# Layer 1's S5 tables: a later start inside layer 0's MLP, and matrix parts that are issued 8 planner units behind their VectorE parts

## The chip, the cores and the metric

The kernel runs on one core of a Trainium2 chip. The metric is the device time of one execution in microseconds. Before the change it is 1744.45 us, the median of three runs (1743.82 to 1749.99). One further execution was recorded by the hardware profiler.

The core's engines run side by side, each through its own list of instructions in order: PE (TensorE, matrix products), DVE (VectorE), ACT (ScalarE), POOL (GpSimd) and SP (SyncE, which here only issues DMAs). They wait for one another through semaphores.

## The reference, cut to what matters

Two layers of a backbone work on 256 latent tokens and 256 context tokens of width 1024. Each layer has a token mixer with four branches, one of which is a bidirectional diagonal state-space mixer (S5), and then an MLP with squared ReLU. Layer 0 computes both token streams, layer 1 the latent one alone. All is in float32.

```python
def sq_relu_mlp(h, w1, w2):                  # w1 1024 x 4096, w2 4096 x 1024
    return jnp.square(jax.nn.relu(h @ w1)) @ w2

def s5_discretize(a_re, a_im, log_dt, b_re, b_im):
    ...
    mag = jnp.exp(lam_re * dt)
    lb_re = mag * jnp.cos(lam_im * dt)       # 16 groups x 64 states, two directions
    lb_im = mag * jnp.sin(lam_im * dt)
    ...
    bb_re = f_re[..., None] * b_re - f_im[..., None] * b_im
    bb_im = f_re[..., None] * b_im + f_im[..., None] * b_re
    return lb_re, lb_im, bb_re, bb_im
...
for l in range(DEPTH):
    mod = jax.nn.silu(c) @ ada_w[l] + ada_b[l]        # adaLN: 1024 x 6144 per layer
    ...
    y, y_c = token_mixer(h, hc, need_ctx, w_in[l], ...)
    x = x + g1 * rms_norm(y, norm_gains[l, 1])
    x = x + g2 * rms_norm(sq_relu_mlp(h, mlp_w1[l], mlp_w2[l]), norm_gains[l, 3])
```

The S5 recurrence runs in blocks of 8 tokens in the kernel. That needs tables, made only from weights: powers of the state factors times B (into the state), powers times C (out of the state), and the response inside a block. They depend on no token and must be in memory when a layer's S5 mixer reads them.

## The kernel before, in words

**Weight tiles.** Every large matrix comes as tiles of 128 x 1024 floats (512 KB). SP loads a tile into `wstage` (three buffers). ACT rounds it to the fast float32r format (`whi`, line 224), DVE computes the rest (`wlo`, line 206), and both are prepared two tiles ahead of their use (four buffers each). PE then runs 24 products of 128 x 128 by 128 x 512 per tile (line 217): 8 blocks of the inner dimension, times three combinations of high and low parts.

**Layer 0's MLP.** Four rounds q = 0 to 3. A round takes 8 tiles of w1 (numbers 8q to 8q+7), whose results pass through `hidden`: ACT makes ReLU, square and the high part, DVE the low part `flo`. Then it takes 8 tiles of w2, whose results DVE adds into `y`. The first four w1 tiles and the last four w2 tiles are done in two halves of 256 columns. Between these, in the fixed list of jobs, stand 48 tiles of `ada_w` for later adaLN vectors: after the first 12 jobs of the stage, 8 ada tiles behind 8 weight tiles, then two weight tiles without. An ada tile is multiplied on DVE by the condition and summed into `aacc` (lines 209 and 213): two operations per tile for layer 0's last part and layer 1's first two parts (24 tiles), one operation per tile for layer 1's other three (24 tiles), by the `conds` of line 406. After each 8 there is a short sum on PE (line 380).

**Side work and its clock.** Small chains of work are Python generators, here `s5_tables(1, ...)` for layer 1. The kernel's author keeps a planner clock. A 512-column weight tile calls `tick` 8 times with 0.648 each, between its blocks. A started generator is resumed at the first tick at which its due time has passed; each resumption adds 0.5 to the clock and sets the due time to the yielded number later. So a yield of 0, 1, 2, 3 or 8 is worth 1, 2, 4, 5 or 13 ticks. This gives the program order. The framework then orders each engine's instructions by that order and by a simulated readiness, so that an instruction whose inputs are there can be moved ahead onto an idle engine. `drain()` runs whatever is left of the generators before the last four w2 tiles.

**The tables of one layer.** `s5_tables` loads B and C (`bct`), makes phases on POOL (`s5_phases`), copies powers on ACT into `pb` and `pc` (line 647), and scales `pb` on DVE. For layer 1 these copies are put behind the instruction `behind` on ACT, which is the ReLU of the w1 tile before the start. Then:

- Four steps make the tables into the state. A step has two halves (real, imaginary): three DVE operations into `raw` (one buffer), four PE transposes (line 679), an ACT copy into `sti` (line 681). Behind the step stands a DMA of 512 KB, then a yield.
- Four steps make the tables out of the state: six small and three large DVE operations and four large POOL operations into `bb` and `sto`, a DMA of 512 KB, a yield; then twice POOL memsets and ACT copies into `ct` and eight PE instructions (line 717), an ACT copy and four small DMAs, a yield.
- At the end 16 gathering loads into `TP` and two stores.

In the kernel before, the generator starts before w1 tile 12.

Of the kernel before, what the change touches and what calls it, by code (L numbers as in the profile page):

```python
# [196 lines left out]
def _emit(tc, I, out):  # L197
# [4 lines left out]
    def act(o, i, f, **k):  # L202
        return S.activation(o, i, f, **k)  # L203

    def tt(o, a, b, op, eng=None):
        return (eng or V).tensor_tensor(o, a, b, op=op)  # L206
# [4 lines left out]
    def ts(o, a, s1, s2, op0, op1=None, eng=None):  # L211
        if op1 is None:
            return (eng or V).tensor_scalar(o, a, s1, None, op0=op0)
        return (eng or V).tensor_scalar(o, a, s1, s2, op0=op0, op1=op1)
# [45 lines left out]
    with es:  # L260
# [53 lines left out]
        def start(gen, delay=0.0, first=False):  # L314
            rec = [gen, clock[0] + delay, first]
            active.append(rec)
            return rec
# [188 lines left out]
        def dense(job, ahi, alo, n):  # L506

            w = next_job(job)
            ps = dense_ps()
            product(ps, w, ahi, alo, 0, n)  # L510
            return ps

        def dense_group(group, ahi, alo, l):

            ws = [next_job(j) for j in group]
            for c0, n, sel in halves(l):
                for i in range(len(ws)):
                    ps = dense_ps()
                    product(ps, ws[i], ahi, alo, c0, n)
                    yield i, sel, ps[:, :n]  # L520
# [108 lines left out]
        def s5_tables(l, tp, keep_in=None, behind=None):  # L629
# [35 lines left out]
            def rank1(o, pw, vec, gs, eng=None):  # L665
                tt(o, pw[:, gs, :, None].to_broadcast([128, 4, 8, 16]),
                   vec[:, gs, None, :].to_broadcast([128, 4, 8, 16]), MUL, eng)
            vb, vc = bcv[:, 0], bcv[:, 1]
            for q in range(4):
                gs = slice(4 * q, 4 * q + 4)  # L670
                raw = tp.tile([128, 2, 4, 8, 16], F32, name="raw", tag="raw")
                sti = tp.tile([128, 4, 2, 128], F32, name="sti", tag="sti", bufs=1 if keep_in is None else 4)
                for ri in range(2):
                    rank1(raw[:, ri], pb[:, 0], vb[:, ri], gs)
                    rank1(t4, pb[:, 1], vb[:, 1 - ri], gs)
                    tt(raw[:, ri], raw[:, ri], t4, (SUB, ADD)[ri])
                    ps = psm.tile([128, 512], F32, name="pm", tag="pm")
                    for g in range(4):
                        PE.transpose(ps[:, 128 * g:128 * g + 128],
                                     raw[:, ri, g].rearrange("p s c -> p (s c)"), ident)  # L680
                    S.copy(sti[:, :, ri], ps.rearrange("p (g m) -> p g m", g=4))
                if keep_in is None:
                    SP.dma_start(s5_dr[l][:, gs, 0:2], sti)
                else:
                    keep_in.append(sti)
                yield 2.0
            for q in range(4):
                gs = slice(4 * q, 4 * q + 4)
                f16 = [a[:, gs, None].to_broadcast([128, 4, 16]) for a in (fr, fi)]
                v1 = t1[:, 0:64].rearrange("p (g c) -> p g c", g=4)  # L690
                tt(bb[:, 0, :, 0:16], vb[:, 0, gs], f16[0], MUL)
                tt(v1, vb[:, 1, gs], f16[1], MUL)
                tt(bb[:, 0, :, 0:16], bb[:, 0, :, 0:16], v1, SUB)
                tt(bb[:, 1, :, 0:16], vb[:, 1, gs], f16[0], MUL)
                tt(v1, vb[:, 0, gs], f16[1], MUL)
                tt(bb[:, 1, :, 0:16], bb[:, 1, :, 0:16], v1, ADD)
                sto = tp.tile([128, 4, 2, 128], F32, name="sto", tag="sto")
                cp = [sto[:, :, i].rearrange("p g (s c) -> p g s c", s=8) for i in range(2)]
                rank1(cp[0], pc[:, 0], vc[:, 0], gs)
                rank1(t4, pc[:, 1], vc[:, 1], gs)  # L700
                tt(cp[0], cp[0], t4, SUB)
                rank1(cp[1], pc[:, 0], vc[:, 1], gs, G)
                rank1(t4b, pc[:, 1], vc[:, 0], gs, G)
                tt(cp[1], cp[1], t4b, ADD, G)
                ts(cp[1], cp[1], -1.0, None, MUL, eng=G)
                SP.dma_start(s5_dr[l][:, gs, 2:4], sto)
                yield 3.0
                ps = psm.tile([128, 512], F32, name="pm", tag="pm")
                for ri in range(2):
                    ct = tp.tile([128, 4, 15, 16], F32, name="ct", tag="ct")  # L710
                    G.memset(ct[0:64, :, 0:7, :], 0.0)
                    G.memset(ct[64:128, :, 8:15, :], 0.0)
                    act(ct[:, :, 7, :], vc[:, ri, gs], AF.Copy, scale=(1.0, -1.0)[ri])
                    S.copy(ct[0:64, :, 8:15, :], cp[ri][0:64, :, 0:7, :])
                    S.copy(ct[64:128, :, 0:7, :], cp[ri][64:128, :, 1:8, :])
                    for g in range(4):
                        PE.matmul(ps[32 * g:32 * g + 32, 0:240], bb[:, ri, g, :],
                                  ct[:, g].rearrange("p i c -> p (i c)"), start=(ri == 0), stop=(ri == 1))
                rsb = tp.tile([128, 240], F32, name="rsb", tag="rsb")
                S.copy(rsb, ps[:, 0:240])  # L720
                for g in range(4):
                    SP.dma_start(r_dr[l][4 * q + g], rsb[32 * g:32 * g + 16])
                yield 1.0
# [641 lines left out]
        SP.dma_start(smp, I["smp"].rearrange("l p n -> p l n"))  # L1365
        maps_in = []
        tables = s5_tables(0, pt, maps_in)
        next(tables)
        first_dma(1)
# [35 lines left out]
        for l in range(L):  # L1405
# [198 lines left out]
            def y_out(n, ps, c0, w, add, last):  # L1604
                o = y[:, n, c0:c0 + w]
                if add:
                    tt(o, o, ps, ADD)
                else:
                    S.copy(o, ps)
                if last:  # L1610
                    a = sqa[:, c0:c0 + w]
                    if n == 0:
                        act(a, o, AF.Square)
                    else:
                        q = px.tile([128, 512], F32, name="sq", tag="sq", bufs=2)
                        act(q[:, :w], o, AF.Square)
                        tt(a, a, q[:, :w], ADD)
# [9 lines left out]
            def hidden(j, ps, c0, w):  # L1627
                r = px.tile([128, 512], F32, name="hr", tag="hr", bufs=2)
                i = act(r[:, :w], ps, AF.Relu)
                r2 = px.tile([128, 512], F32, name="hq", tag="hq", bufs=2)  # L1630
                act(r2[:, :w], r[:, :w], AF.Square)
                split(fhi[:, j, c0:c0 + w], flo[:, j, c0:c0 + w], r2[:, :w])
                return i
# [16 lines left out]
            for q in range(4):  # L1650
                j0 = 0
                if q == 0:
                    j0 = g2
                    for i, sel, ps in dense_group([("w1", l, n) for n in range(g2)], hhi, hlo, l):
                        hidden(i, ps, 256 * sel, 256)
                for j in range(j0, 8):
                    if l == 0 and 8 * q + j == 12:
                        pt = Pool("pt1")
                        start(s5_tables(1, pt, None, gate))
                    gate = hidden(j, dense(("w1", l, 8 * q + j), hhi, hlo, nq)[:, :nq], 0, nq)  # L1660
                for n in range(8 - g3 if q == 3 else 8):
                    y_out(n, dense(("w2", l, 8 * q + n), fhi, flo, nq)[:, :nq], 0, nq, q > 0, q == 3)
# [28 lines left out]
```

## Time and profile before

| | us |
|---|---|
| median of the three runs | 1744.45 |
| the profiled execution | 1743.24 |
| its span from first to last instruction | 1741.4 |
| PE busy in the span | 1596.5 |
| DVE busy | 1083.1 |
| ACT busy | 796.8 |
| POOL busy | 219.9 |
| mean granted TensorE clock, share of full speed | 0.961 |

Times in the trace count from the start of the span. An engine's busy time is the sum of its instructions' times; a PE matmul's end is modelled, so PE's pace is better read from starts. "idle before" and the name behind an arrow say what ended an engine's idle time. PEclk is the granted TensorE clock of a stretch: 1.00 is 2.4 GHz, 0.50 would be 1.2 GHz all through, and a value between is a mixture of the two.

### The profile page before, as it was taken

The page shows a single profiled execution, that of the slowest core. Times are in us where ns is not written, and L with a number is a line of the kernel's source. Part 1 is how long each engine was busy: PE and PEld are TensorE (multiplying, and loading weights), DVE is VectorE, ACT ScalarE, POOL GpSimd, SP SyncE. Part 2 cuts the span into 40 slices and gives each one's busy share as a digit, 9 for nine tenths or more (in the row PEclk, how much of TensorE's full clock was granted, in tenths as well). Part 3 has the DMA queues.
Part 4 walks back from the last instruction along what each step waited for, and adds up shares of the span by engine and source line. Part 5 has one row for each costly group of instructions (what it writes and reads, how often), then busy time and mean ns, then how long its engine had stood idle before and what let it go on. Part 6 is the DMA issues. An engine that isn't in the chain of part 4 may idle for free.

```text
span 1741.4 us, 25278 instructions
## 1 busy us (share of the span) xinstructions
PE 1596.5 (92%) x9560; PEld 1320.0 (76%) x9560; DVE 1083.1 (62%) x1943; ACT 796.8 (46%) x1488; POOL 219.9 (13%) x316
## 2 busy tenths in 40 slices
PE   6699999999999798998799999889999887789996
PEld 2588767766778687876568888778888787779996
DVE  8765644475537668758844546684567675565554
ACT  5444455533334355524324244534775340556553
POOL 6730000000002373001310000100000030000000
PEclk9799999999999898999899999999999997889998
DMA  8446543554346532545565653436635550447552
GB/s 318 148 135 207 170 124 94 142 162 115 99 157 219 168 110 85 169 159 168 160 176 166 197 160 129 149 111 187 201 117 182 144 166 8 138 140 230 188 183 85
DMA packets 135913, 268.41 MB, mean 154 GB/s; under 512 B 38128, under 2 KB 76016, under 8 KB 135664
## 3 DMA queue, kind: packets, MB, share of 16 engines
q1 hardware_dynamic: 135792, 266.80, 48.9%
q8 instruction: 75, 1.23, 0.3%
q14 instruction: 46, 0.38, 0.1%
HBM read 234.02 MB, written 32.74 MB: 153 GB/s over the span
## 4 chain that ended last, share of the span: by engine, by line
PE 75%; DVE 12%; DMA 6%; ACT 3%; issue 3%; POOL 1%; SPq 0%; POOLq 0%; ACTq 0%; DVEq 0%
PE pd L217 39%; PE pm L217 23%; PE pg L217 9%; DVE wlo L206 2%; DMA wstage<-in_ada 1%; DMA wstage<-in_w 1%; DMA gin<-g_dr 1%; PE pm L833 1%; ACT whi L224 1%; PE pd L380 1%; DVE hlo L209 1%; DVE aacc L209 1%; DVE raw L206 1%; DVE gin L209 1%; DVE cv L209 1%
## 5 line engine op out<-in xcount | busy, mean ns | idle before, releaser
L206 DVE TENSOR_TENSOR wlo<-wstage,whi 128x1024 fp32r<-128x1024 f32 x264 | 327.1, 1241 | 257.6 <-ACT whi L224 240.7
L224 ACT CAST whi<-wstage 128x1024 fp32r<-128x1024 f32 x264 | 276.2, 1048 | 411.8 <-PE pd L217 163.3
L217 PE MATMUL pd<-hhi,whi 128*128 128x256 f32 (+1 forms) x1184 | 408.3, 346 | 20.9 <-ACT us L1425 11.1
L217 PE MATMUL pd<-hlo,whi 128*128 128x256 f32 (+1 forms) x1184 | 404.0, 342 | 5.7 <-DVE hlo L209 5.7
L217 PE MATMUL pd<-hhi,wlo 128*128 128x256 f32 (+1 forms) x1184 | 402.5, 341 | 1.3 <-DVE wlo L206 1.3
L217 PEld LDWEIGHTS pd<-hhi,whi 128*128 128x128 f32 x1184 | 225.3, 191 | 63.3 <-issue 13.4
L217 PEld LDWEIGHTS pd<-hlo,whi 128*128 128x128 f32 x1184 | 225.6, 191 | 38.6 <-issue 8.7
L217 PEld LDWEIGHTS pd<-hhi,wlo 128*128 128x128 f32 x1184 | 225.5, 191 | 31.7 <-issue 7.1
L217 PE MATMUL pm<-hhi,whi 128*128 128x256 f32 (+1 forms) x352 | 116.1, 331 | 6.3 <-ACT hhi L203 6.3
L217 PE MATMUL pm<-hlo,whi 128*128 128x256 f32 (+1 forms) x352 | 115.6, 329 | 3.9 <-DVE hlo L209 3.9
L209 DVE SCALAR_TENSOR_TENSOR aacc<-wstage,csl,aacc 128x1024 f32<-128x1024 f32 x70 | 88.6, 1284 | 46.2 <-DMA wstage<-in_ada 45.9
L217 PE MATMUL pm<-hhi,wlo 128*128 128x256 f32 (+1 forms) x352 | 114.9, 327 | 0.3 <-DVE wlo L206 0.3
L217 PE MATMUL pd<-fhi,wlo 128*128 128x256 f32 (+1 forms) x272 | 90.9, 334 | 2.8 <-DVE wlo L206 2.8
L217 PE MATMUL pd<-fhi,whi 128*128 128x256 f32 (+1 forms) x272 | 90.9, 335 | 2.5 <-DVE y L206 1.4
L217 PE MATMUL pm<-fhi,wlo 128*128 128x256 f32 (+1 forms) x272 | 89.6, 330 | 1.2 <-DVE wlo L206 1.2
L217 PE MATMUL pm<-fhi,whi 128*128 128x256 f32 (+1 forms) x272 | 90.1, 331 | 0.7 <-ACT fhi L224 0.7
L217 PE MATMUL pd<-flo,whi 128*128 128x256 f32 (+1 forms) x272 | 90.6, 333 | 0.0
L217 PE MATMUL pm<-flo,whi 128*128 128x256 f32 (+1 forms) x272 | 89.5, 329 | 0.0
L217 PEld LDWEIGHTS pm<-hhi,whi 128*128 128x128 f32 x352 | 68.7, 195 | 14.0 <-ACT hhi L203 8.0
L217 PEld LDWEIGHTS pm<-hlo,whi 128*128 128x128 f32 x352 | 68.1, 194 | 10.2 <-DVE hlo L209 4.8
L217 PEld LDWEIGHTS pm<-hhi,wlo 128*128 128x128 f32 x352 | 68.2, 194 | 6.0 <-DVE wlo L206 0.5
L1174 POOL MEMSET N<- 32x1024 f32 x8 | 7.6, 946 | 431.4 <-DMA n_dr<-N 222.9
(588 smaller groups left out, 2917.8 us busy)
## 6 DMA issues: line engine op xcount, KB each, us to landing
wstage<-in_w SPq DMA_DIRECT2D x128, 512.0 KB, 4.2
wstage<-in_win SPq DMA_DIRECT2D x104, 512.0 KB, 4.0
wstage<-in_ada SPq DMA_DIRECT2D x80, 512.0 KB, 3.6
ada<-in_ada SPq DMA_DIRECT2D x16, 512.0 KB, 10.5
g_dr<-gt SPq DMA_DIRECT2D x32, 256.0 KB, 3.1
gin<-g_dr SPq DMA_DIRECT2D x16, 512.0 KB, 4.1
wstage<-in_wb SPq DMA_DIRECT2D x16, 512.0 KB, 4.2
wstage<-in_wout SPq DMA_DIRECT2D x16, 512.0 KB, 3.6
```

The costliest lines, as they stand in the source:

```text
L206: return (eng or V).tensor_tensor(o, a, b, op=op)
L209: return (eng or V).scalar_tensor_tensor(o, a, s, b, op0=op0, op1=op1)
L217: return PE.matmul(o, l, r, start=st, stop=sp)
L224: S.copy(hi, src)
L380: PE.matmul(ps[32 * q:32 * q + 32, 0:256], lhs, w[:, 256 * q:256 * q + 256], start=st, stop=sp)
L833: PE.transpose(ps[:, 128 * b:128 * b + 128], P[qt][:, 128 * b:128 * b + 128], ident)
L1174: G.memset(Nf[32 * b:32 * b + 32, :, 32 * b:32 * b + 32], 0.0)
```

## The change

Three edits. The generator for layer 1 starts before w1 tile 18 instead of 12; between them lie 4 w1 tiles, 8 w2 tiles and 2 w1 tiles, and the ada tiles among these. In the steps into the state, for layer 1 alone (`behind` is given), a yield of 8.0 stands between the DVE operations of each half and its transposes. In the steps out of the state the yield between the DVE and POOL part and the PE part is 8.0 instead of 3.0, for layer 1 alone. Layer 0's tables are as before.

```diff
@@ s5_tables, into the state, for each half ri
                     rank1(raw[:, ri], pb[:, 0], vb[:, ri], gs)
                     rank1(t4, pb[:, 1], vb[:, 1 - ri], gs)
                     tt(raw[:, ri], raw[:, ri], t4, (SUB, ADD)[ri])
+                    if behind is not None:
+                        yield 8.0
                     ps = psm.tile([128, 512], F32, name="pm", tag="pm")
                     for g in range(4):
                         PE.transpose(ps[:, 128 * g:128 * g + 128],
@@ s5_tables, out of the state
                 SP.dma_start(s5_dr[l][:, gs, 2:4], sto)
-                yield 3.0
+                yield 3.0 if behind is None else 8.0
                 ps = psm.tile([128, 512], F32, name="pm", tag="pm")
@@ layer 0's MLP
                 for j in range(j0, 8):
-                    if l == 0 and 8 * q + j == 12:
+                    if l == 0 and 8 * q + j == 18:
                         pt = Pool("pt1")
                         start(s5_tables(1, pt, None, gate))
                     gate = hidden(j, dense(("w1", l, 8 * q + j), hhi, hlo, nq)[:, :nq], 0, nq)
```

## Rows read from the trace of the kernel before

**Rows 1.** The page: busy time (share, instructions) by engine, then the ending chain by engine.

```profile
PE 1596.5 (92%) x9560; PEld 1320.0 (76%) x9560; DVE 1083.1 (62%) x1943; ACT 796.8 (46%) x1488; POOL 219.9 (13%) x316
...
PE 75%; DVE 12%; DMA 6%; ACT 3%; issue 3%; POOL 1%; SPq 0%; POOLq 0%; ACTq 0%; DVEq 0%
```

**Rows 2.** Windows: length, busy (count) of PE, PEld, DVE, ACT, POOL, PEclk, DMA, GB/s.

```profile
780.00:790.00 10.00, 10.00 (x45) 8.23 (x44) 7.28 (x7) 5.34 (x8) 0.00 (x0) 1.00 0.72 238
820.00:830.00 10.00, 1.19 (x5) 0.72 (x4) 9.88 (x12) 1.17 (x2) 0.00 (x0) 0.68 0.80 256
830.00:840.00 10.00, 8.34 (x27) 6.80 (x28) 9.14 (x16) 0.59 (x1) 0.00 (x0) 0.64 0.50 159
1090.00:1100.00 10.00, 7.66 (x54) 6.20 (x54) 10.00 (x24) 4.83 (x13) 3.17 (x4) 1.00 0.57 205
```

**Rows 3.** Timeline of PE: start, us, instruction, count, [idle before it and releaser].

```profile
827.74 1.09 PE L679 MATMUL pm<-cst,raw 128*128 128x128 f32 x4 [7.64 <-DVE raw L206]
```

**Rows 4.** Timeline of DVE in the same stretch.

```profile
823.31 1.28 DVE L209 SCALAR_TENSOR_TENSOR aacc<-wstage,csl,aacc 128x1024 f32<-128x1024 f32 x1
...
825.71 1.28 DVE L209 SCALAR_TENSOR_TENSOR aacc<-wstage,csl,aacc 128x1024 f32<-128x1024 f32 x1
826.90 0.68 DVE L206 TENSOR_TENSOR raw<-raw,t 128x512 f32<-128x512 f32 x1
```

**Rows 5.** Windows of line 217 alone: length, PE and PEld busy (count), PEclk.

```profile
796.02:902.51 106.49, 76.42 (x291) 56.49 (x289) 0.90 0.55 167
902.51:1058.79 156.28, 155.28 (x672) 126.12 (x673) 1.00 0.55 173
706.42:1058.79 352.37, 320.37 (x1346) 254.59 (x1346) 0.97 0.55 173
```

**Rows 6.** Timeline of PE around the tables' instructions.

```profile
809.07 0.39 PE L217 MATMUL pd<-hhi,whi 128*128 128x512 f32 x1
809.30 0.60 PE L679 MATMUL pm<-cst,raw 128*128 128x128 f32 x4
809.65 0.48 PE L217 MATMUL pd<-hlo,whi 128*128 128x512 f32 x1
...
846.35 0.40 PE L217 MATMUL pd<-fhi,wlo 128*128 128x512 f32 x1
846.68 0.61 PE L717 MATMUL pm<-ct,bb 128*32 128x240 f32 x8
847.22 0.51 PE L217 MATMUL pm<-fhi,whi 128*128 128x512 f32 x1
```

**Rows 7.** Windows of line 380 alone (the ada sums).

```profile
796.02:902.51 106.49, 2.46 (x32) 0.73 (x32) 0.90 0.55 167
706.42:1058.79 352.37, 4.81 (x64) 1.46 (x64) 0.97 0.55 173
```

**Rows 8.** Windows of all engines over three parts of the stage.

```profile
706.42:796.02 89.60, 89.60 (x400) 72.40 (x400) 58.33 (x59) 35.50 (x53) 0.00 (x0) 1.00 0.57 181
796.02:902.51 106.49, 86.42 (x419) 62.65 (x417) 81.22 (x110) 40.15 (x72) 30.75 (x30) 0.90 0.55 167
902.51:1058.79 156.28, 156.28 (x692) 126.44 (x689) 80.63 (x86) 58.95 (x82) 0.00 (x0) 1.00 0.55 173
```

**Rows 9.** Lines of DVE, 797 to 892: instructions xcount | busy us, mean ns | idle before.

```profile
L206 DVE TENSOR_TENSOR flo<-hq,fhi 128x512 fp32r<-128x512 f32 x5 | 5.3, 1074 | 0.0
```

**Rows 10.** Windows of the tile sto alone: length, busy (count) of DVE, ACT, POOL.

```profile
796.02:902.51 106.49, 7.23 (x8) 8.98 (x16) 19.33 (x12) 0.90 0.55 167
```

**Rows 11.** Lines of DVE, 902.6 to 1058.

```profile
L206 DVE TENSOR_TENSOR flo<-hq,fhi 128x512 fp32r<-128x512 f32 x16 | 10.9, 688 | 4.1 <-ACT fhi L224 4.1
```

**Rows 12.** Timeline of POOL: the first phase operation of layer 1.

```profile
615.51 0.66 POOL L612 COPY ph<-s5u 128x8 f32<-128x8 f32 x1
```

**Rows 13.** Timeline of ACT at the start of layer 1's tables.

```profile
797.43 0.60 ACT L647 COPY pc<-s5l 64x128 f32<-64x128 f32 x2
```

**Rows 14.** The chain that ended last, in time: start, us, what.

```profile
1168.92 3.43 DMA s5s<-s_dr
```

## The prediction

> **What bounds the kernel now.** I read the page's busy times and its ending chain first, then the stage that the change touches in windows, then the instructions in it. PE is busy for 92% of the span and holds 75% of the chain that ended last [rows 1], so time is won only where PE stands or runs slowly. In layer 0's MLP the reader is to see two pictures. Around the tables PE is full: in 780 to 790 it is busy 10.00 of 10 us at clock 1.00 while DVE has 7.28 [rows 2]. In 820 to 830 PE has 1.19 us and DVE 9.88, and the granted clock is 0.68, then 0.64 in the next ten [rows 2]: PE stood, and part of the following stretch ran at 1.2 instead of 2.4 GHz. The instructions say why: at 827.74 PE's transposes had waited 7.64 us for `raw` [rows 3], whose last subtraction DVE did only at 826.90, behind a row of `aacc` operations of 1.28 us [rows 4]. PE's list is in order, so every weight tile behind the transposes stood too.
>
> **How much is lost there.** The stretch 796.02 to 902.51 holds the tables of layer 1. It has 291 weight matmuls; the calm stretch behind it has 672 in 155.28 us, 0.2311 us each [rows 5]. So 291 would take 67.2 us. To that come the tables' own PE work and the ada sums. Four transposes push the next matmul from 0.23 to 0.58 us behind the one before them (809.07 to 809.65), so 0.35 us, eight times: 2.8. A group of line 717 pushes it from 0.23 to 0.87 (846.35 to 847.22), so 0.64, eight times: 5.1 [rows 6]. The ada sums have 2.46 [rows 7]. Together 77.6; the stretch took 106.49, so 28.9 us are lost. As a cross-check the whole stage from w1 tile 4 to w2 tile 27 took 352.37 with 1346 matmuls [rows 5]: 311.1, plus 7.9 for the tables and 4.81 [rows 7], leaves 28.6. So nothing else in the stage loses time, and about 29 us is the ceiling of this change there.
>
> **Why it is lost: DVE's room.** In 706.42 to 796.02, 16 tiles (384 matmuls), DVE was busy 58.33 us without tables [rows 8], 3.65 a tile of 5.60, so 1.95 are free. In 796.02 to 902.51 it had 81.22 [rows 8] for 291/24 = 12.1 tiles; less 12.1 x 3.65 the tables took 37 us. Of these 24 operations on `raw` of 0.68 [rows 4] are 16.3, and 20.7 are for `pb`, `bb` and `sto`. The generator's old yields come to 1 + 2 + 4 ticks, then 4 x 4, 4 x (5 + 2) and 5: 56 ticks, 7 tiles. Seven tiles have 14 us of room for 37 us of work. A step into the state comes every 4 ticks, half a tile or 2.8 us, and needs 4.1 us of DVE; its transposes are issued right behind it.
>
> **The change part by part.** *The later start.* From w1 12 to w1 18 are 14 tiles of 5.58 us (156.28/28), so the tables begin near 875. The stretch from 902.51 is w1 16 to w2 27, 28 tiles, and DVE was busy 80.63 us in it [rows 8]: 2.88 a tile, because an ada tile is one DVE operation there instead of two. 2.70 us a tile are free. The old place is left with what 706 to 796 had, where PE had work in all 89.60 us [rows 8], so I expect no loss there: the cover is the two tiles prepared ahead, and without it a late DVE would cost what [rows 3] shows.
>
> *The yields into the state.* The new sums are 1 + 2 + 4 ticks, then 4 x (13 + 13 + 4) = 120: 15 tiles for the four steps. Room 15 x 2.70 = 40 us for 16.3 plus `pb`. A half has 2.0 us of DVE work and 13 ticks, 1.6 tiles or 9 us, before PE asks for it. The wait of [rows 3] goes. What is late next on PE is the next weight tile, which ACT and DVE prepare two tiles ahead. Behind the later transposes stand ACT's copy `sti`, SP's store and the next `raw` (one buffer); none is on PE's path as long as a half's 9 us hold.
>
> *The yields out of the state.* Four times 13 + 2 ticks, 60: 7.5 tiles, room 20.3 us against at most 20.7. This just fills DVE, though two of these tiles (w1 28 and 29) have no ada tile. Here I book what is left: the price lies between 0 and the whole excess if DVE and POOL hinder each other more (below, up to 14 us). Instructions that share the time with POOL are already long in these sums: `flo` had 1074 ns among the tables [rows 9] and 688 in the calm stretch [rows 11]. The 20.7 contain this, so I take 3 us, near the lower end.
>
> *What moves along.* 42 DMAs of the tables on SP (4 + 4 stores of 512 KB, 16 small, 16 gathers, 2 stores) and `bct` and two phase stores. Their 10 large stores and the gathers' loads are some 6.5 MB, over 24 tiles (134 us) 48 GB/s beside 173 [rows 8], an estimate of 221, below the 256 that one window moved [rows 2]. A store that SP must wait for delays the weight loads queued behind it; one such stop costs nothing to 7.6 us if it reaches PE, as the longest stop did [rows 3]. A gain is excluded, since PE is always busy where the weights come now [rows 8]. I take nothing: by the estimate the DMA engines have room. The phases on POOL ran at 615.51 [rows 12], 180 us ahead of their place, and should again; moved back they would meet an idle POOL. The ACT copies that open the rest started at 797.43 [rows 13] and follow the new gate.
>
> *The end.* 1 + 2 + 4 + 120 + 60 + 5 = 192 ticks, 24 tiles: the last step falls at w2 26, two full tiles ahead of the `drain()`, near 1017. The S5 mixer of layer 1 waited for table loads at 1168.92 [rows 14], some 1143 then. Nothing is late there.
>
> **The sum.** 28.9 saved, 3 given back: 26 us. Against the profiled execution, 1743.24 - 26 = 1717 us; that execution lies 1.2 below the median of 1744.45, which changes nothing in what follows.
>
> **POOL and DVE.** In the tables' stretch POOL's three operations on `sto`, four times, took 19.33 us and DVE's eight took 7.23 [rows 10], 0.90 each instead of 0.68 [rows 4]. So they hinder each other, by a third, not fully. The Trainium skill (SBUF — State Buffer, Who interferes with whom) says that a VectorE instruction with two SBUF inputs and a GpSimd instruction that reads SBUF exclude each other for a whole instruction, and that the issue order decides who stands. By that rule `wlo` and `flo` would stand behind POOL as well, which no yield changes; the trace agrees in direction (`flo`, above) but shows far less than all of POOL's time lost on DVE. By it the time would be that of the second case below.
>
> **The rivals.**
> 1. *The forecast:* the stall goes, 0 to 6 us come back as small waits: 1712 to 1724.
> 2. *DVE is full in the part out of the state.* If DVE stood for all of POOL's 19.33 us, it would need 20.7 + 19.3 = 40 us where 20.3 are free. One tile of lead (5.6) hides some, 14 reach PE: 1743.24 - 29 + 14 = 1728. For it: that part fills DVE even by my count. Against: the 7.23 for eight operations.
> 3. *The stall is not the tables' order, or the order on the engines isn't the program's.* The scheduler moves work far ahead [rows 12]; it could pack the DVE halves and transposes as closely as before, or the two-operation ada tiles of w2 8 to 15 stop DVE without tables. Then the 29 us stay: 1743. Against: with the same ada load, 706 to 796 lost nothing.
> 4. *Slower: the end slips behind the `drain()`.* If the steps out of the state are over 7.5 tiles late, they fall into the stretch before layer 1, where DVE is busy 10.00 of 10 us and PE waits on it (7.66) [rows 2]. Then each of their DVE microseconds counts, and PE's matrix parts wait for POOL: 20.7 + 19.3 = 40 against 29 saved: 1754. It decides from a delay of 9.5 tiles, two of reserve and the 7.5; DVE has 43 us of room ahead of it, so I hold it unlikely.
>
> **How the numbers follow.** Chances 0.62, 0.18, 0.12 and 0.08. The likeliest gives 1717. Its own range and the second's reach from 1712 to some 1735; I take 1710 to 1735, with 2 us below for a schedule that falls better, and leave out the third and fourth, two in ten. A measurement of this kernel tells a change of 0.5%, 8.7 us, from none: faster is below 1735.7, so the first two cases and a little of the third, 0.81; within, 0.11; slower, 0.08.
>
> **What would show it.** Right: no PE idle time before line 679 beyond 1 us; PE busy at clock 1.00 from 796 to some 875 and DVE at 6 to 7 of 10 there; the copies of line 647 near 875 and the last line 717 before 1032; DVE 8 to 10 of 10 in the last eight tiles of the tables. Wrong: PE waits for `wlo` or `y` while `sto` and `bb` run (the second case), PE stops again in 820 to 870 without tables (the third), line 717 or 679 behind w2 27 (the fourth). A change outside this stage of over 5 us would mean that the scheduler rearranged other work, for which I have no term.

## The result and the profile after

The changed kernel takes 1725.95 us, the median of four runs (1723.21 to 1726.99), beside 1744.13 us for the kernel before in the same measurement. The ratio is 0.9894 with a 95% interval of 0.9857 to 0.9931, so it is faster by 12 to 25 us. The forecast was 1717, in a range of 1710 to 1735: the side and the range hold, the size does not. The profiled execution took 1726.2 us, with a span of 1724.4 where the kernel before had 1741.4. In the changed kernel the lines behind the first new yield are shifted by two: the transposes are line 681, the matrix groups out of the state line 719.

The page's busy times and the shares of the chain that ended last, for the changed kernel; they answer to [rows 1].

```profile
PE 1596.2 (93%) x9560; PEld 1322.4 (77%) x9560; DVE 1083.6 (63%) x1943; ACT 809.5 (47%) x1497; POOL 222.7 (13%) x316
...
PE 77%; DVE 10%; DMA 7%; ACT 4%; issue 2%; POOL 0%; SPq 0%; POOLq 0%; ACTq 0%; DVEq 0%
```

PE, DVE and POOL do the same instructions as before, DVE 1083.6 us beside 1083.1; their idle time is less. ACT has nine instructions and 12.7 us more: nine more loads of its function tables, 1.28 us each, stand at 1200 to 1225 in layer 1, where the framework put other instructions in another order. That part lies far behind the stage of the change, and from the first 512-column product of layer 1 to the end of the span the changed kernel takes 628.7 us beside 630.0, so they cost nothing that shows. The windows show where the time was won. The columns are those of [rows 2]: length, then busy time (count) of PE, PEld, DVE, ACT and POOL, PEclk, DMA share, GB/s.

```profile
796.00:876.00 80.00, 80.00 (x358) 64.29 (x357) 45.49 (x47) 25.47 (x33) 0.00 (x0) 1.00 0.49 154
...
820.00:830.00 10.00, 10.00 (x55) 7.69 (x50) 9.44 (x11) 3.03 (x5) 0.00 (x0) 1.00 0.45 140
830.00:840.00 10.00, 10.00 (x44) 8.04 (x44) 9.38 (x10) 2.10 (x2) 0.00 (x0) 1.00 0.76 236
...
1010.00:1020.00 10.00, 10.00 (x54) 7.04 (x54) 6.85 (x8) 5.48 (x10) 5.07 (x5) 1.00 0.99 265
1020.00:1030.00 10.00, 7.04 (x30) 5.28 (x29) 6.94 (x12) 2.64 (x5) 1.77 (x3) 1.00 0.78 221
1030.00:1040.00 10.00, 9.05 (x43) 7.53 (x44) 4.34 (x6) 3.46 (x6) 0.93 (x2) 0.66 0.65 205
```

In the tables' old place PE is now full at clock 1.00, where [rows 2] had 1.19 us of 10. But a new hole has come at 1020 to 1040: PE at 7.04 of 10, then ten microseconds at a granted clock of 0.66, a mixture of 1.2 and 2.4 GHz. The stage as a whole is the next view, line 217 alone (length, PE and PEld busy, PEclk, DMA share, GB/s), as in [rows 5].

```profile
708.02:874.00 165.98, 164.12 (x710) 132.90 (x709) 1.00 0.54 169
874.00:1026.40 152.40, 145.53 (x613) 113.64 (x611) 1.00 0.62 194
1026.40:1042.56 16.16, 11.38 (x50) 9.70 (x49) 0.79 0.55 170
708.02:1042.56 334.54, 321.03 (x1371) 256.24 (x1369) 0.99 0.58 180
```

The prediction's own sum, made again for the last row: 1346 products at 0.2311 are 311.1 us; 25 products of 256 columns at 0.12 are 3.0; the tables have 7.9 and the ada sums 4.5. That is 326.5 of 334.5, so 8 us are still lost, where the kernel before lost 28.6. The stage gained 20.6 us. The span gained 17.0: w1 tile 4 started 1.8 us later in this execution (708.02 beside 706.25), and the rest lies behind the stage. Both are of the size that executions of one program differ by: w1 tile 4 started between 704.4 and 711.9 in the kernels below, none of which changes anything ahead of it.

The PE waits of the whole stage, 708 to 1042.5, are three (total us, times, longest).

```profile
PE pd L217 <- DVE y L206: 2.7, 1, 2.7
PE pd L217 <- DVE wlo L206: 1.2, 1, 1.2
PE pm L681 <- DVE raw L206: 0.4, 1, 0.4
```

The wait of 7.64 on `raw` [rows 3] is down to 0.37. The other two belong to the new hole, which PE's timeline shows.

```profile
1026.18 0.39 PE L217 MATMUL pd<-fhi,wlo 128*128 128x512 f32 x1
1029.30 0.36 PE L217 MATMUL pd<-fhi,whi 128*128 128x256 f32 x1 [2.73 <-DVE y L206]
1029.50 0.27 PE L217 MATMUL pd<-flo,whi 128*128 128x256 f32 x1
1030.95 0.58 PE L217 MATMUL pd<-fhi,wlo 128*128 128x256 f32 x1 [1.17 <-DVE wlo L206]
1031.33 0.42 PE L217 MATMUL pd<-fhi,whi 128*128 128x256 f32 x1
...
1035.60 0.41 PE L217 MATMUL pd<-fhi,wlo 128*128 128x256 f32 x1
1035.94 1.01 PE L719 MATMUL pm<-ct,bb 128*32 128x240 f32 x8
1036.88 0.50 PE L217 MATMUL pm<-fhi,whi 128*128 128x512 f32 x1
...
1042.77 0.61 PE L719 MATMUL pm<-ct,bb 128*32 128x240 f32 x8
```

The shapes matter here. Products of 256 columns belong to the last four w2 tiles, which come behind w2 27 in the program. Here 24 of them, one half of w2 28, stand ahead of the 512-column products of w2 27 (from 1036.88), and behind them the first half of the tables' last step (line 719 at 1035.94; the second half comes at 1042.77). PE starts them 2.73 us late, waits once more for that tile's `wlo`, and then runs them 0.21 us apart instead of the 0.12 they have at full clock: 24 x 0.09 is 2.2 more. With 2.73, 1.17 and the slow line 719 (1.01 instead of 0.61) that is about 6.5 of the 8 us. DVE's timeline shows what it did meanwhile.

```profile
1027.27 1.28 DVE L209 SCALAR_TENSOR_TENSOR aacc<-wstage,csl,aacc 128x1024 f32<-128x1024 f32 x1 [2.71 <-DMA wstage<-in_ada]
1028.47 0.68 DVE L206 TENSOR_TENSOR y<-y,pd 128x512 f32<-128x512 f32 x1
1029.07 0.68 DVE L206 TENSOR_TENSOR t<-pc,bct 128x512 f32<-128x512 f32 x1
1029.67 1.22 DVE L206 TENSOR_TENSOR wlo<-wstage,whi 128x1024 fp32r<-128x1024 f32 x1
```

An `aacc` waits 2.71 us for an ada load, and the `y` that frees PE's `pd` buffer stands behind it. So from the trace alone there are two readings: a late load, or a list of PE that asks for `y` and `wlo` too early. The experiments had to tell them apart.

### The profile page after: what moved, and what is told of

It is laid out like the page before. It is cut to its first block, busy times and chain, and to the rows that moved or that the text cites. A ratio compares the mean times of both kernels' runs of the same rounds, so it can differ in the third digit from the quotient of the medians.

```text
span 1724.4 us, 25280 instructions
## 1 busy us (share of the span) xinstructions
PE 1596.2 (93%) x9560; PEld 1322.4 (77%) x9560; DVE 1083.6 (63%) x1943; ACT 809.5 (47%) x1497; POOL 222.7 (13%) x316
## 4 chain that ended last, share of the span: by engine, by line
PE 77%; DVE 10%; DMA 7%; ACT 4%; issue 2%; POOL 0%; SPq 0%; POOLq 0%; ACTq 0%; DVEq 0%
PE pd L217 41%; PE pm L217 23%; PE pg L217 9%; DVE wlo L206 2%; DMA wstage<-in_w 2%; DMA wstage<-in_ada 2%; DMA gin<-g_dr 1%; PE pm L835 1%; ACT whi L224 1%; PE pd L380 1%; ACT L203 1%; DVE hlo L209 1%; DVE cv L209 1%; DVE aacc L209 1%; DVE gin L209 1%
## 5 line engine op out<-in xcount | busy, mean ns | idle before, releaser
L217 PE MATMUL pd<-hhi,whi 128*128 128x256 f32 (+1 forms) x1184 | 411.1, 349 | 22.0 <-ACT us L1427 11.1
L217 PEld LDWEIGHTS pm<-hlo,whi 128*128 128x128 f32 x352 | 67.0, 190 | 10.5 <-DVE hlo L209 4.8
```

What stands on the lines that cost most here:

```text
L217: return PE.matmul(o, l, r, start=st, stop=sp)
```

## The experiments

Three measurements of four kernels each were made, every one beside the kernel before (1746.14, 1746.47 and 1745.73 us). "Stage" reaches further here than in the sum above: it is the time from the first product of w1 tile 4 to the first product of layer 1 in the profiled execution; it leaves out the scatter of the rest. The kernel before has 383.35 there. "Start" is the w1 tile before which the tables begin.

| kernel | start | yields in the steps | median us | ratio, 95% interval | stage us |
|---|---|---|---|---|---|
| the change | 18 | into and out of | 1725.95 | 0.9894 [0.9857, 0.9931] | 363.2 |
| the change again (a_again) | 18 | both | 1724.53 | 0.9869 [0.9838, 0.9900] | 361.4 |
| s18_old | 18 | none | 1748.06 | 1.0021 [1.0005, 1.0038] | 385.2 |
| s12_new | 12 | both | 1721.35 | 0.9867 [0.9842, 0.9892] | 355.4 |
| s12_raw | 12 | into | 1727.59 | 0.9890 [0.9863, 0.9916] | 366.3 |
| s12_out | 12 | out of | 1731.44 | 0.9905 [0.9874, 0.9936] | 371.6 |
| s18_nogather | 18 | both | 1721.84 | 0.9871 [0.9847, 0.9894] | 360.6 |
| s18_nopool | 18 | both | 1720.80 | 0.9867 [0.9845, 0.9888] | 358.1 |
| s18_pg | 18 | both | 1719.30 | 0.9834 [0.9795, 0.9873] | 357.1 |
| s16_new | 16 | both | 1718.22 | 0.9848 [0.9818, 0.9878] | 357.7 |
| s14_new | 14 | both | 1718.36 | 0.9837 [0.9800, 0.9875] | 355.7 |
| s20_new | 20 | both | 1724.13 | 0.9870 [0.9832, 0.9907] | 369.0 |
| s24_new | 24 | both | 1740.34 | 0.9973 [0.9953, 0.9993] | 387.4 |

### The late start alone, the spread alone

The change has two parts: a later start and longer yields. Each was done alone. The late start with the old yields (s18_old) is the changed kernel without the new yields:

```diff
-                    if behind is not None:
-                        yield 8.0
...
-                yield 3.0 if behind is None else 8.0
+                yield 3.0
```

Expected: 

> The late start alone (w1 tile 18, the old yields of 2 and 3). Room theory (VectorE's free time in the tiles that the steps span decides): the steps span 7 tiles with 2.70 us free each, 19 us for 37 us of work, against 14 before; the missing time falls from 23 to 18 us, so some 23 of the 29 us of loss stay, time about 1738 us, and TensorE waits for raw again by several us. Rival (the place alone decides, because an ada tile is one VectorE operation there): about 1726, as with the whole change, and no wait for raw.

The spread with the old start (s12_new):

```diff
-                    if l == 0 and 8 * q + j == 18:
+                    if l == 0 and 8 * q + j == 12:
```

Expected: 

> The spread alone (start at w1 tile 12 as before, the new yields of 8). Room theory: the 15 tiles of the steps into the state have some 12 x 1.95 + 3 x 2.70 = 31 us free for about 20, so no wait for raw and the 29 us go as with the late start. If the 6.7 us that the changed kernel loses at 1026 to 1037 come from the end of the tables lying against the last w2 tiles, they go too: about 1719 us. If they come from the gathering loads wherever these stand (loads late, three stage buffers), a stop of some us appears 6 tiles earlier: 1724 to 1726. Rival (the place decides): about 1740, with waits for raw in 820 to 870.

Measured: the late start alone gains nothing, 1748.06 at a ratio of 1.0021. The stop moves with the tables. Windows of s18_old in their new place:

```profile
900.00:920.00 20.00, 10.69 (x43) 7.18 (x42) 17.37 (x29) 4.25 (x7) 0.00 (x0) 0.66 0.59 188
```

PE has 10.69 of 20 us there, and its waits from 870 to 1062 are led by these.

```profile
PE pd L217 <- DVE wlo L206: 6.9, 2, 4.4
PE pm L679 <- DVE raw L206: 6.0, 4, 2.1
```

The spread alone gains everything that was to be had: 27.9 us in the stage, which is the ceiling that the prediction worked out (28.6 to 28.9), and PE has not one wait between 700 and 1031. The median of the whole time falls by 24.8 us. The stretch 820 to 840, first of the kernel before, then of s12_new, is the most telling pair of rows in this case.

```profile
820.00:840.00 20.00, 9.52 (x32) 7.52 (x32) 19.03 (x27) 1.76 (x3) 0.00 (x0) 0.66 0.65 208
```

```profile
820.00:840.00 20.00, 20.00 (x94) 16.18 (x91) 19.93 (x25) 5.50 (x8) 0.00 (x0) 1.00 0.69 218
```

DVE is even fuller with the spread, 19.93 of 20 us beside 19.03, and PE loses nothing. A full DVE was not what stopped PE. It stood because its transposes were in its list before DVE had come to their `raw`. With the spread DVE comes to them in time. The third half's last `raw` operation on DVE and its transposes on PE, in s12_new:

```profile
829.42 0.68 DVE L206 TENSOR_TENSOR raw<-raw,t 128x512 f32<-128x512 f32 x1
...
835.06 0.60 PE L681 MATMUL pm<-cst,raw 128*128 128x128 f32 x4
```

`raw` is ready 5.0 us ahead of PE here, and 1.9 us ahead in the first half, 10.5 in the second and 5.0 to 7.3 in the halves 3 to 6. The yields there do two things at once: they put a distance of about 9 us between the two parts, and they stretch the tables over more weight tiles. No run separates them; the same yields behind the transposes would. By an estimate from these times 2 to 4 of the 9 us were used up in the halves 3 to 6, so transposes right behind their `raw` would still have waited there.

### Which yield

Old start, one yield each:

```diff
 # s12_raw
+                    if behind is not None:
+                        yield 8.0
 # s12_out
-                yield 3.0
+                yield 3.0 if behind is None else 8.0
```

Expected of the yield into the state: 

> Old start before w1 tile 12, with the yield of 8.0 in the steps into the state alone; the steps out of the state keep 3.0. In the kernel before, 796.02 to 846.35 (into the state) holds 132 weight matmuls: 30.5 us at 0.2311, 2.8 for transposes and 1.2 for the ada sum, so 15.8 of its 50.3 are lost; 846.35 to 902.51 holds 160: 37.0 + 5.1 + 1.2, so 12.9 of 56.2 are lost. Theory that each part loses by its own crowding: this kernel gains 15 to 16, about 1729, and PE still stops in the part out of the state. Theory that the part out of the state only pays for a backlog that the part into the state leaves on DVE: all 28 are gained, about 1718 to 1721, and no PE stop over 1 us is left.

Expected of the yield out of the state: 

> Old start before w1 tile 12, with the yield of 8.0 in the steps out of the state alone; no yield inside the halves of the steps into the state. Theory that each part loses by its own crowding: this kernel gains the 13 us of the part out of the state, about 1731, and PE still waits 5 to 10 us for raw. Theory that the part out of the state only pays for a backlog of the other: it gains less than 13, 1735 to 1744, because the backlog still arrives and is only stretched; then the yield into the state does all the work of the change.

Measured: 17.1 us of the stage for the first and 11.8 for the second, where 15.8 and 12.9 were expected. Together 28.9, and both in one kernel gain 27.9. So each part loses by its own crowding, and there is no backlog that one leaves to the other. The waits that stay are those of the untouched part. PE's timeline in s12_raw:

```profile
935.39 0.79 PE L217 MATMUL pd<-fhi,wlo 128*128 128x512 f32 x1 [4.38 <-DVE wlo L206]
```

And in s12_out:

```profile
826.07 1.09 PE L679 MATMUL pm<-cst,raw 128*128 128x128 f32 x4 [7.63 <-DVE raw L206]
830.16 1.09 PE L679 MATMUL pm<-cst,raw 128*128 128x128 f32 x4 [3.00 <-DVE raw L206]
```

The 7.63 is [rows 3] again, to a hundredth: with the yields into the state gone the old stop is back.

### The hole at 1026: gathers, POOL, or the order

Two kernels take away a load that stands at the place of the hole. s18_nogather leaves out the 16 gathering loads into `TP` for layer 1 (a memset stands for them); s18_nopool leaves out the four operations with which POOL makes the imaginary half of `sto` in each step (a memset stands for them).

```diff
 # s18_nogather
-                for s in range(8):
+                if behind is not None:
+                    G.memset(TP, 0.0)
+                for s in range(8 if behind is None else 0):
 # s18_nopool
+                if behind is None:
                     rank1(cp[1], pc[:, 0], vc[:, 1], gs, G)
                     ...
+                else:
+                    G.memset(cp[1], 0.0)
```

Expected without the gathers: 

> The changed kernel without the 16 gathering loads of layer 1's last table (a POOL memset fills the tile instead; the stores stay). Theory that the stop at 1026 to 1037 comes from the weight loads: in 1010 to 1020 the DMA engines were busy at 0.99 and SP waited for the gathers before it issued the next loads; without them no wait of VectorE on an ada load above 1.5 us there, no half clock, 6 to 7 us faster than the changed kernel: about 1719. Rival (VectorE and POOL hinder each other): no change, about 1726.

Expected without POOL's operations: 

> The changed kernel without POOL's four operations of each step out of the state for layer 1 (one memset of the imaginary part instead). Theory that POOL's work holds VectorE back and so makes the stop at 1026 to 1037: stop gone, about 1719 us, flo near 0.69 us each instead of 0.85. Rival (loads late because of the gathers): the stop stays, within 2 us of 1726, though the flo times fall all the same.

Measured: 1721.84 and 1720.80 us, ratios of 0.9871 and 0.9867. In both, PE still waits for `y` and `wlo` (2.0 and 0.6; 1.0 and 1.2 us), and the 256-column products still stand ahead of w2 27. The hole is smaller but not gone. How little that says was seen only when the changed kernel itself was measured again:

Expected of it: 

> The changed kernel once more, unaltered, beside three variants. If the stop of its last tables (PE waits 2.73 us for y at 1029 and then runs at half clock) is a property of the program, this run shows it again in the same place, line 217 stands there for over 3 us in all, and the time is about 1726, 4 to 6 us above the kernel with the spread alone. If the stop was an accident of one execution, no wait over 1 us stands between 1000 and 1045 and the time is about 1720.

It took 1724.53, with the hole in the same place but smaller, in PE's timeline:

```profile
1016.71 0.50 PE L217 MATMUL pm<-flo,whi 128*128 128x512 f32 x1 [1.06 <-DVE flo L206]
...
1025.94 0.36 PE L217 MATMUL pd<-fhi,whi 128*128 128x256 f32 x1 [1.00 <-DVE y L206]
1027.58 0.58 PE L217 MATMUL pd<-fhi,wlo 128*128 128x256 f32 x1 [1.17 <-DVE wlo L206]
```

So the hole belongs to the program, and its size differs between executions by about as much as the two experiments had moved it. Whether gathers and POOL have a share in its size stays open; neither makes it alone, since it is there without either.

The order was tried next. Every second weight tile uses a PSUM buffer of the pool `pm`, and so do the tables. The next kernel takes the tables' buffers out of the state from the pool `pg` of the ada sums and leaves all else as it is in the change:

```diff
                 yield 3.0 if behind is None else 8.0
-                ps = psm.tile([128, 512], F32, name="pm", tag="pm")
+                if behind is None:
+                    ps = psm.tile([128, 512], F32, name="pm", tag="pm")
+                else:
+                    ps = psg.tile([128, 512], F32, name="pg", tag="pg")
```

Expected: 

> The change with one edit: the PSUM tile of the steps out of the state (layer 1) comes from the pool with the tag pg, which the ada sums use, instead of pm, which every second weight tile uses. In the changed kernel's list for PE 24 products of 256 columns of w2 28 and the last line 719 stand ahead of the 24 products of w2 27, which need a pm buffer behind that last step; in this kernel's list all products of 512 columns come first. Start, yields and all the work are as in the change. Theory that the stop of the changed kernel (PE waits for y and wlo at 1026 to 1031, then half clock) comes from this order: no wait over 1 us before the last 512-column product, the stage from w1 4 to there takes 326 to 328 us instead of 333 to 334, time about 1719. Rival, that the ada loads are late on DVE at this place whatever PE's order is: PE still waits 2 to 4 us for y or wlo there, the stage stays at 331 to 334, time about 1725.

Measured: 1719.30. PE has no wait at all between 700 and 1031, and its timeline runs from the last 512-column product into the first of 256 without a break. Two groups out of the state now come behind.

```profile
1030.66 0.40 PE L217 MATMUL pd<-fhi,wlo 128*128 128x512 f32 x1
1030.90 0.28 PE L217 MATMUL pm<-fhi,whi 128*128 128x256 f32 x1
...
1033.05 0.61 PE L722 MATMUL pg<-ct,bb 128*32 128x240 f32 x8 [1.52 <-issue]
```

DVE still waited for an ada load, at the same fill of the DMA engines (240 and 283 GB/s in 1010 to 1030), but not for the same one. An ada group has eight tiles; these are the fifth operation of line 209 in the last group, and the seventh. DVE's timeline in s18_pg:

```profile
1016.48 1.29 DVE L209 SCALAR_TENSOR_TENSOR aacc<-wstage,csl,aacc 128x1024 f32<-128x1024 f32 x1 [3.39 <-DMA wstage<-in_ada]
...
1028.91 1.29 DVE L209 SCALAR_TENSOR_TENSOR aacc<-wstage,csl,aacc 128x1024 f32<-128x1024 f32 x1
```

In the change the fifth waited 3.12 us, at 1014.27, and cost PE nothing there either. The one in the hole is the seventh, which waited 2.71; here it does not wait. So s18_pg took away both the order and that late load, and does not part the two readings by itself. The start before w1 tile 16, in the next section, does: there the seventh is late and PE loses nothing. In the change, w2 27 takes its `pm` buffer in one rotation with the tables' last step; the framework put half of w2 28 ahead of both, and PE asked for that half before DVE had it ready. With the tables' buffers in another pool the order is gone. Which of the three `pm` buffers held w2 27 back in the framework's reckoning was not followed. The stage is 4 to 6 us shorter than in the change's two executions. The ratio 0.9834 [0.9795, 0.9873] and the change's own two overlap at their ends, so on the whole time the gain is likely, not proved.

### Where the tables end

The same hole should go if the tables end before the last tiles, and worse should come if they end behind them.

```diff
-                    if l == 0 and 8 * q + j == 18:
+                    if l == 0 and 8 * q + j == 16:      # and 14, 20, 24
```

Start 16: 

> Both spreads as in the change, start before w1 tile 16 instead of 18: the tables end two weight tiles (11 us) earlier, still among the last w2 tiles. Theory that the stop comes from the end falling on the last four w2 tiles, whose 256-wide products take weight tiles at twice the pace: two tiles are enough, no PE wait over 1 us between 1000 and 1045, the stage gains 26 to 28 us, time about 1720. Theory that the last part of the stage is bad as such for the part out of the state (single-operation ada tiles, one load per operation, DMA engines at 0.99): the stop moves 11 us forward with the tables and stays at 4 to 7 us, time about 1726.

Start 14: 

> The change with the start before w1 tile 14 instead of 18: the tables end four weight tiles earlier than with 16... that is, the 8 w2 tiles between 15 and 16 all lie behind the start, so the end falls on w2 18 instead of w2 26. Both theories of the stop (PE's order at the drain, late ada loads at the drain) say that there is none: the stage takes 324 to 327 us, as with the starts 12 (324.6) and 16 (326.5), and the time is 1718 to 1721. If it is over 1724, the place inside the stage matters in a way that neither has.

(The tile that this names as the end is wrong: 24 tiles from w1 14 end near w2 21.)

Start 20: 

> The change with the start before w1 tile 20 instead of 18: the last step out of the state and the gathers fall into the last four w2 tiles (two of the line 719 groups stand among the 256-column products). By the price of the fourth case in the prediction (20.7 us of DVE and 19.3 of POOL for four steps, 10 a step, all of it on the path behind the drain) one to two steps cost 10 to 20 us more than the gain left: 1727 to 1737. Rival: behind the drain PE has tiles ready and the steps hide there too: 1722 to 1726, as the change.

Start 24: 

> The change with the start before w1 tile 24: the fourth case of the prediction in full, all steps out of the state and part of those into it stand behind the drain, among the last four w2 tiles. By its price (29 saved, 40 us of DVE and POOL in the open) the time is about 1754, 10 above the kernel before; with the 10 us of DVE into the state that slip behind it as well up to 1764. If DVE's and POOL's work there is hidden to a half, 1735 to 1740. Under 1730 would mean that the stretch behind the drain is no bad place at all and that the fourth case had no price.

Measured: with the starts 16 and 14 all 512-column products come first again, PE's waits in the stage are 0.7 and 0.5 us and none, and the times are 1718.22 and 1718.36, the lowest medians. They beat the kernel before clearly; against the change the intervals overlap. In s16_new the seventh ada operation waits longer than in the change, and two `y` stand behind it; yet PE is full. DVE's timeline, then the windows of all engines:

```profile
1029.23 1.28 DVE L209 SCALAR_TENSOR_TENSOR aacc<-wstage,csl,aacc 128x1024 f32<-128x1024 f32 x1 [3.65 <-DMA wstage<-in_ada]
1030.43 0.68 DVE L206 TENSOR_TENSOR y<-y,pm 128x512 f32<-128x512 f32 x1
```

```profile
1020.00:1040.00 20.00, 20.00 (x104) 15.40 (x103) 11.22 (x13) 8.88 (x14) 0.94 (x2) 1.00 0.67 196
```

So the late load alone makes no hole; it takes PE's order. Whether the order alone would make one is not shown: in all five executions that have it (the change twice, s18_nogather, s18_nopool, s20_new) the seventh load was late too, by 2.4 to 3.8 us.

Start 20 took 1724.13, as the change and not 1727 to 1737, with the change's order and waits (2.7 us for `y`, 0.6 for `wlo`). Start 24, the fourth case of the prediction in full, took 1740.34: not 1754, but most of the gain is gone. PE's waits in s24_new from 1026 to 1075, and the windows of all engines in the worst part:

```profile
PE pm L719 <- issue: 11.1, 2, 6.5
PE pm L719 <- POOL t L206: 6.5, 1, 6.5
PE pm L719 <- POOL ct L714: 3.0, 2, 1.5
PE pm L719 <- ACT ct L717: 0.5, 1, 0.5
```

```profile
1040.00:1070.00 30.00, 9.05 (x68) 4.71 (x69) 17.06 (x25) 10.01 (x23) 21.38 (x23) 0.60 0.43 126
```

PE has 9.05 of 30 us while POOL works for 21.38 of them: there the tables stand in a chain of POOL, ACT and PE with no weight tile to fill it. For 11.1 us of these waits the profile names no releaser. The stage in the table overstates the loss of s20_new and s24_new: the late tables move the product at which it ends. From there to the first 512-column product of layer 1 these two take 17 us, all others 22 to 26. Measured up to that product, the start 20 has 386.1 us beside 387.7 and 385.5 of the change, and the start 24 has 404.4, which is 23 us longer than the spread with the old start (381.1) and 0.7 shorter than the kernel before (405.1).

## Why the prediction was right, and where it was off

**The ceiling.** 28.9 us were put down as lost. The spread with the old start gained 27.9 in the stage. Right, and so is the split by part that was worked out from the same trace ahead of its runs (15.8 and 12.9 expected, 17.1 and 11.8 measured). The median of the whole time fell by 24.8 us there.

**The yields into the state.** Right: 0.37 us of wait instead of 7.64, and the yield alone, at the old start (s12_raw), takes these waits away. The reason given, nine microseconds between a half and its transposes, fits the times of s12_new above, but the yield also stretches the steps, and no run has the one without the other.

**The later start and DVE's room.** Off. The prediction took the room per tile for the cause, 1.95 us free in the old place and 2.70 in the new. The late start alone gained nothing, and with the spread the old place, with less room, has the shorter stage (355.4 beside 363.2 and 361.4; in the whole time the intervals overlap). The spread decides: 24 tiles in either place have more than the 37 us that the tables need, and the two parts stand apart. Where the tables stand decides nothing as long as it is not the end.

**The old place.** Right: PE is full from 796 to 876 and DVE has 45.49 of 80 us, 5.7 of 10 where 6 to 7 was put.

**The yields out of the state, 3 us given back.** Up to the hole the price was nothing: between 985 and 1025 DVE is busy 32.58 of 40 us, within the 8 to 10 of 10 that were put, and PE all 40.00. The second case gave 1728, close to what was measured, and its sign was met in the letter: PE waited for `y` and `wlo` while the last step's `t` and `sto` were on DVE. The mechanism is another, so the closeness is luck. Ahead of that wait DVE was not full but stood 2.71 us for a load, POOL worked 1.77 of the ten microseconds from 1020, and without POOL's operations PE waited 1.0 and 1.2 us there, just as in the second execution of the change.

**The end: "Nothing is late there".** This is the step that failed. The prediction counted ticks, found two tiles of reserve ahead of the drain and looked only at who reads the tables later. The last line 719 came at 1042.77 and not before 1032, behind w2 27's last 512-column product, which was the sign of the fourth case without its price; and the tables' PSUM buffers, shared with the weight tiles, turned PE's order at the drain around. That is the hole of some 6.5 us, with the other small losses 8, where 3 were booked: 5 of the 9 us between forecast and measurement. The other 4 lie ahead of the stage (1.8) and behind it, within what executions differ by. A PSUM rotation appears nowhere in the prediction's list of what a moved step takes with it.

**What moves along.** The estimate of 221 GB/s was for the mean over the tables' tiles; 194 were moved there (874 to 1026.4). Single stretches had more (265 in 1010 to 1020, the engines 0.99 busy), and loads were late on DVE. That reached PE only together with the order above. POOL's phases ran early again (617.08), and the copies of line 647 followed the gate (877.45), as written.

**The slower case.** Late tables do lose, but about half of what was put: the start 24 takes 22 us more than the starts 16 and 14, not 40, and so it stays 5 us below the kernel before (1740.34 beside 1745.73), where 10 above it was forecast.

## What to carry to other kernels

When an in-order engine stands for a helper's result, first ask how far ahead the result was queued, and only then how busy its maker is: here DVE at 19.93 of 20 us cost nothing once its part was issued eight planner units before PE's and the tables were spread over more tiles. When side work is moved, list the buffers that it shares with the main work and look where the last of them is taken: a rotation of PSUM buffers can turn the order of the main engine at the next seam, and here starting two tiles earlier, or another pool, cost nothing.

## What the runs showed of the hardware

POOL's work stretches DVE's. Between 985 and 1025 the changed kernel's DVE has these rows (count, busy us, mean ns, idle before):

```profile
L209 DVE SCALAR_TENSOR_TENSOR aacc<-wstage,csl,aacc 128x1024 f32<-128x1024 f32 x6 | 9.5, 1587 | 3.4 <-DMA wstage<-in_ada 3.4
...
L206 DVE TENSOR_TENSOR flo<-hq,fhi 128x512 fp32r<-128x512 f32 x5 | 5.1, 1022 | 1.6 <-ACT fhi L224 1.6
...
L206 DVE TENSOR_TENSOR bb<-bct,s5f 128x64 f32<-128x64 f32 x5 | 2.2, 431 | 0.0
```

Without POOL's four operations (s18_nopool) the same stretch has:

```profile
L209 DVE SCALAR_TENSOR_TENSOR aacc<-wstage,csl,aacc 128x1024 f32<-128x1024 f32 x7 | 9.0, 1283 | 8.6 <-DMA wstage<-in_ada 8.6
...
L206 DVE TENSOR_TENSOR flo<-hq,fhi 128x512 fp32r<-128x512 f32 x5 | 3.4, 689 | 2.2 <-ACT fhi L224 2.2
...
L206 DVE TENSOR_TENSOR bb<-bct,s5f 128x64 f32<-128x64 f32 x5 | 1.1, 213 | 0.9 <-PE pm L722 0.9
```

All three kinds are shorter: `aacc` has the 1.28 us of [rows 4] again, `flo` falls from 1022 to 689 ns, beside the 688 of [rows 11], and `bb` from 431 to 213. DVE's busy time falls from 32.58 to 24.90 us, by 7.7, while POOL's falls from 20.40 to 5.74, by 14.7: DVE lost about half of the time that POOL worked. The Trainium skill (SBUF — State Buffer, Who interferes with whom) says that a VectorE instruction with two SBUF inputs and a GpSimd instruction that reads SBUF contend with each other. The runs agree with it: the instructions that grew here all have two such inputs, and the one-input `aacc` of line 213 took 753 ns in both. PE was at 40.00 of 40 us in both, so in this stretch the price stayed on DVE.

The second surprise is how one program's executions differ. The changed kernel's two profiled executions took 1726.2 and 1720.7 us with the same instructions; their hole at 1026 was 2.73 and 1.00 us at its first wait. A wait of 2 us read in one trace is within that, and only the repeat showed it.
